# A hybrid transformer block on one core: its first stage as one pass over the input in blocks of k, and keys and queries put in place by ScalarE and VectorE

## The chip, the cores and the metric

One core of a Trainium2 chip runs the whole block; the other cores are idle. The metric is the device time of one execution in microseconds (us), and the median of several executions is compared. The engines are named as the profile names them: PE is TensorE's matmul, PEld its weight load, DVE is VectorE, ACT is ScalarE, POOL is GpSimd, SP is SyncE, which here only issues DMAs.

## The reference

One layer over 512 tokens of width 1024, batch 1, float32. Cut to what matters here:

```python
h = rms_norm(x, ln1_g)                       # x: 512 x 1024
z = h @ w_in                                 # 1024 x 3368; split into
# mq mk mv mo (512 each), mi mf (4 each), aq (512), akc avc aks avs akw avw (128 each), ag (24)
hm = mlstm(mq, mk, mv, mi + b_i, mf + b_f)   # 4 heads, gates by cumulative sums and maxima
m_out = rms_norm(hm) * sigmoid(mo)
# nsa: Kc = gelu(blocks(akc) + pos @ w1) @ w2, the same for Vc from avc (31 blocks of 32 tokens, stride 16);
# softmax attention over (Kc, Vc), over selected blocks (aks, avs) and over a window (akw, avw),
# 8 query heads in 2 groups, mixed by sigmoid(ag)
a_out = nsa(aq, akc, avc, aks, avs, akw, avw, ag, ...)
x = x + concat([m_out, a_out]) @ w_out
x = x + conv_ffn(rms_norm(x, ln2_g), w_up, conv_w, conv_b, w_down)
x = x + sigmoid(rms_norm(x) @ w_ple_gate) * (p @ w_ple_proj)
return rms_norm(x, final_g)
```

## The kernel before

Every matrix product of float32 data runs as three products of a high and a low part (`hi` by ACT `Copy` to fp32r, `lo` by a DVE subtraction): x-high by w-high, x-low by w-high, x-high by w-low. So each weight block that lands needs one ACT and one DVE instruction before TensorE can use it.

The activations stand transposed: eight blocks `k` of 128 features by 512 tokens (`x1h`, `x1l`). The work is a queue of jobs (`Stream`): a job loads a weight block (`split`, L119 to L126: a DMA on SP into one of two `raw` buffers, then hi, then lo), and its matmuls are written out while the next job's block is prepared. `st.after(us, fn)` writes a piece of other work (statistics, transposes, evacuations) after so many us of TensorE work have been written. A scheduler then fixes the order of instructions on each engine, and each engine runs its list strictly in that order.

The stages that the change touches, by their first matmul in the profile:

- `tok0` to `tok3` (L300, L301, L305): token-major products of 288 columns (v of two branches, gate inputs), a job for two blocks of k; the x blocks land and are split while these run. Then the squares and their sum `acc`, the statistics matmuls `n1ps` (L262), ten small DVE instructions (`newton_rsqrt`, L244 to L254), and `n1pb` (L281), which spreads the reciprocal norm over the columns as `rb1`.
- `c0`, `k0`, `c1` (L355, L356, L359): the feature-major products for akc, aks, avc, each 24 matmuls of 512 columns, one job each.
- `k1`, `q00`, then `cw00` (L434 to L439, the first layer of the compression, 24 small matmuls), `q01`, `cw01`, `mv0`, `cw10`, `mv1`, `cw11`, `mv2`, `mv3`: the order is the string `ORDER`. `pgt` (L579) and `pgc` (L600) are transposes for the mLSTM gates, whose chain of small operations runs over DVE and ACT (`mlstm_gates`, L579 to L593).
- Then the first scores (`s_3b`, L661) and the attention, into which `q10`, `q11`, `mo`, `mq` are filled; later the mLSTM heads, `w_out`, the FFN, the gate and the last norm.

A key or query has to stand twice, hi and lo, in rows of 64. `key_evac` and `q_evac` make hi and lo at 128 rows (L383, L384) and move the halves to their places by DMAs on POOL's queue (`move`, L388): 12 for the keys, 24 for the queries. `cmp_evac` shifts the two streams of the compression by one token through four DMAs on ACT's queue each (L411, L412) and adds the positions in four DVE sums (L418).

Of the kernel before, what the change touches and what calls it, by code (L numbers as in the profile page):

```python
# [39 lines left out]
GATES = "k0"  # L40
AHEAD = (1, 1)
# [25 lines left out]
def hybrid_block_kernel(ctx: ExitStack, tc: tile.TileContext, a, out):  # L67
# [40 lines left out]
    xbuf = main.tile([128, KB, S], F32, tag="B16", bufs=3, name="xT")  # L108
# [8 lines left out]
    def split(name, src_ap, shape):  # L117
        raw = wpool.tile(shape, F32, tag="raw", bufs=2, name=name + "r")
        hi = wpool.tile(shape, F32R, tag="hi", name=name + "h")  # L119
        lo = wpool.tile(shape, F32R, tag="lo", name=name + "l")  # L120
        n = 1 if name == "tok0" else shape[1]
        for i in range(0, shape[1], n):
            nc.sync.dma_start(raw[:, i:i + n], src_ap[:, i:i + n])
            SE.activation(hi[:, i:i + n], raw[:, i:i + n], AF.Copy)
            VE.tensor_sub(lo[:, i:i + n], raw[:, i:i + n], f32(hi[:, i:i + n]))
        return hi, lo  # L126

# [5 lines left out]
    class Stream:  # L133


        def __init__(self):
            self.jobs, self.ready, self.cur, self.done = [], [], None, set()
            self.now, self.events, self.debt = 0.0, [], 0.0
# [18 lines left out]
        def step(self):  # L157
            if self.cur is None:
# [5 lines left out]
                self.prepare(AHEAD[self.now > 100])  # L164
# [147 lines left out]

    psA = four("ptm")
    for c in range(4):
        st.add(f"tok{c}", a["w_tok"][:, 2 * c:2 * c + 2], [128, 2, 288], tokens_job(psA, 2 * c, 288))
    nc.sync.dma_start(cols, a["cols"])
    nc.sync.dma_start(xbuf[:, 0], a["xT"][:, 0])
    st.prepare(1)
    nc.sync.dma_start(xbuf[:, 1], a["xT"][:, 1])
    for c in range(4):  # L320
        if c < 3:
            nc.sync.dma_start(xbuf[:, 2 * c + 2:2 * c + 4], a["xT"][:, 2 * c + 2:2 * c + 4])
        for k in (2 * c, 2 * c + 1):
            last = SE.activation(xh[:, k], xbuf[:, k], AF.Copy, scale=cols[:, C_G1 + k:C_G1 + k + 1])
            VE.scalar_tensor_tensor(xl[:, k], xbuf[:, k], cols[:, C_G1 + k:C_G1 + k + 1], f32(xh[:, k]),
                                    op0=ALU.mult, op1=ALU.subtract)
        st.until(f"tok{c}")
        if c == 0:
            load_consts()
# [47 lines left out]
    mixa = main.tile([128, 2, 4, S], F32R, tag="mixa", name="mixa")  # L377
# [12 lines left out]
    def key_evac(br):  # L390
        def evac(ps):
# [832 lines left out]
```

## Time and profile before

| | us |
|---|---|
| median of 3 runs | 652.57 (648.09 to 653.72) |
| the profiled execution | 649.89 |
| its span, first to last instruction | 648.1 |
| PE busy in it | 621.4 (96%), 3090 matmuls |
| DVE, ACT, POOL busy | 422.3, 312.0, 51.8 |
| mean granted TensorE clock | 0.991 |

The profile is one execution. The span is 1.8 us less than the time of that execution. Busy shares are means over stages with different limits, so the stages are read one by one: the rows below begin with the whole and then go by stretches whose ends are the starts of a first matmul (5.75 `tok0`, 22.07 `c0`, 43.84 `k1`, 67.10 `mv0`, 95.71 the first scores).

### The profile page before, as it was taken

How to read it: one execution, taken by the hardware profiler on the slowest of the kernel's cores; microseconds unless marked ns; L12 is line 12 of the kernel's file. 1: busy time of each engine (PE TensorE's matmuls, PEld its weight loads, DVE VectorE, ACT ScalarE, POOL GpSimd, SP SyncE). 2: the span in 40 equal slices, each digit the busy share in tenths (PEclk: the TensorE clock that was granted, in tenths of full speed). 3: DMA queues.
4: the chain of work that ended last, by engine and by line, in shares of the span. 5: the costliest groups of instructions: out<-in, count | busy, mean ns of one | idle time of the engine just before them, and what ended most of it. 6: DMA issues, size and time to landing. Idle time of an engine off the chain costs nothing.

```text
span 648.1 us, 8626 instructions
## 1 busy us (share of the span) xinstructions
PE 621.4 (96%) x3090; PEld 506.6 (78%) x3090; DVE 422.3 (65%) x862; ACT 312.0 (48%) x650; POOL 51.8 (8%) x114
## 2 busy tenths in 40 slices
PE   6899899999999999999999999999999999999993
PEld 6788677777777777777878888888888888888892
DVE  4697548888877977685786555555555334346766
ACT  5544346677757656555545343433333323233642
POOL 1213104211111100000000000000000000000003
PEclk9999899999999999999999999999999999999997
DMA  7776945511211152113223323233233333333203
GB/s 226 183 177 159 217 130 114 115 33 33 66 36 63 34 195 89 42 34 97 66 97 98 97 98 98 98 98 98 98 98 98 98 97 98 98 99 108 87 2 129
DMA packets 22083, 64.85 MB, mean 100 GB/s; under 512 B 2832, under 2 KB 6032, under 8 KB 21844
## 3 DMA queue, kind: packets, MB, share of 16 engines
q1 hardware_dynamic: 18120, 57.55, 28.2%
q0 software_dynamic: 3136, 5.57, 4.7%
q10 hardware_dynamic: 784, 1.18, 0.7%
q8 instruction: 24, 0.39, 0.2%
q14 instruction: 19, 0.16, 0.1%
HBM read 56.42 MB, written 2.10 MB: 90 GB/s over the span
## 4 chain that ended last, share of the span: by engine, by line
PE 77%; DVE 10%; DMA 6%; ACT 4%; issue 2%; SPq 0%; DVEq 0%; POOL 0%; ACTq 0%
PE pu L355 8%; PE pu L359 8%; PE pu L356 8%; PE pd L355 5%; PE pd L356 5%; PE pd L359 5%; PE pt L711 2%; PE pmq L356 2%; DMA xT<-in_xT 2%; PE pmq L355 2%; PE pmq L359 2%; PE pv L719 1%; PE mo L889 1%; PE pg L347 1%; PE pg L348 1%
## 5 line engine op out<-in xcount | busy, mean ns | idle before, releaser
L1002 ACT ACTIVATE u<-zv 128x512 fp32r<-128x512 f32 x16 | 10.1, 633 | 45.3 <-DVE zv L1000 45.3
L714 ACT ACTIVATE ph<-pt 128x512 fp32r<-128x512 f32 x40 | 23.6, 597 | 16.4 <-PE pt L711 15.8
L999 DVE TENSOR_TENSOR zv<-pu,n2rb 128x512 f32<-128x512 f32 x16 | 11.1, 691 | 31.3 <-PE pu L359 31.3
L715 DVE TENSOR_TENSOR pl<-pt,ph 128x512 fp32r<-128x512 f32 x40 | 27.1, 684 | 6.3 <-ACT ph L714 6.0
L684 POOL TENSOR_SCALAR E<-E,rr 128x512 f32<-128x512 f32 (+3 forms) x32 | 20.4, 637 | 128.0 <-DVE rr L681 79.4
L989 DVE TENSOR_TENSOR zg<-pu,n2rb 128x512 f32<-128x512 f32 x16 | 11.1, 692 | 26.0 <-PE pu L359 24.6
L711 PE MATMUL pt<-ident,E 128*128 128x128 f32 x160 | 27.4, 274 | 0.4 <-DVE E L686 0.3
L1015 DVE TENSOR_TENSOR X<-pd,X 128x512 f32<-128x512 f32 x8 | 5.5, 691 | 31.9 <-PE pd L359 31.9
L711 PEld LDWEIGHTS pt<-ident,E 128*128 128x128 f32 x160 | 20.0, 140 | 6.7 <-DVE E L686 2.1
L992 ACT ACTIVATE cv<-zg,cols 128x512 f32<-128x512 f32 x16 | 13.1, 816 | 20.1 <-DVE zg L989 20.1
L678 ACT ACTIVATE E<-s,nm 128x384 f32<-128x384 f32 (+2 forms) x48 | 22.1, 470 | 0.0
L995 ACT ACTIVATE cv<-cv 128x512 f32<-128x512 f32 x16 | 10.1, 631 | 24.6 <-DVE cv L994 24.6
L988 POOL MEMSET zg<- 128x2 f32 x16 | 1.5, 99 | 244.0 <-DVE cv L994 151.0
L235 DVE TENSOR_TENSOR acc<-acc,sq 128x512 f32<-128x512 f32 (+1 forms) x30 | 19.1, 636 | 1.6 <-ACT sq L231 1.0
L719 PE MATMUL pv<-ph,V 128*128 128x512 f32 x40 | 18.7, 468 | 0.4 <-ACT ph L714 0.4
L231 ACT ACTIVATE sq<-X 128x512 f32<-128x512 f32 (+1 forms) x24 | 13.5, 560 | 11.0 <-DVE X L1056 11.0
L347 PE MATMUL pg<-x3h,wres 128*128 128x256 f32 x64 | 18.3, 285 | 0.0
L348 PE MATMUL pg<-x3l,wres 128*128 128x256 f32 x64 | 18.1, 283 | 0.0
L349 PE MATMUL pg<-x3h,wres 128*128 128x256 f32 x64 | 18.1, 283 | 0.0
L1003 DVE TENSOR_TENSOR u<-zv,u 128x512 fp32r<-128x512 f32 x16 | 11.1, 692 | 10.5 <-ACT u L1002 10.5
L1096 POOL TENSOR_TENSOR X<-X,n40rb 128x256 f32<-128x256 f32 (+1 forms) x5 | 4.8, 994 | 155.5 <-ACT n40rb L284 155.5
L721 PE MATMUL pv<-pl,V 128*128 128x512 f32 x40 | 16.7, 417 | 0.0
(1079 smaller groups left out, 2041.1 us busy)
## 6 DMA issues: line engine op xcount, KB each, us to landing
Q<-hlq POOLq DMA_DIRECT2D x24, 128.0 KB, 5.4
X<-in_xT SPq DMA_DIRECT2D x1, 2048.0 KB, 7.7
wgr<-in_w_pg SPq DMA_DIRECT2D x4, 512.0 KB, 4.0
xT<-in_xT SPq DMA_DIRECT2D x3, 512.0 KB, 6.4
K<-hlk POOLq DMA_DIRECT2D x12, 128.0 KB, 4.7
out_y<-X SPq DMA_DIRECT2D x5, 256.0 KB, 2.1
out_y<-X SPq DMA_DIRECT2D x5, 128.0 KB, 1.7
Q<-in_qaug POOLq DMA_DIRECT2D x2, 272.0 KB, 7.3
```

The source lines that it names most:

```text
L235: return VE.tensor_add(acc[:, :n], acc[:, :n], sq[:, :n])
L347: TE.matmul(ps, wh[:, kw], rh[:, kx, n], start=first, stop=False)
L348: TE.matmul(ps, wh[:, kw], rl[:, kx, n], start=False, stop=False)
L355: TE.matmul(ps, wh[:, w], rh[:, x, n], start=first and j == 0, stop=False)
L356: TE.matmul(ps, wh[:, w], rl[:, x, n], start=False, stop=False)
L359: TE.matmul(ps, wl[:, w], rh[:, x, n], start=False, stop=last and j == len(kx) - 1)
L678: SE.activation(e, p, AF.Exp, bias=nm[:, b:b + 1], accum_out=rs[:, b:b + 1])
L684: GE.tensor_scalar(e, e, rr[:, b:b + 1], 0.0, op0=ALU.mult, op1=ALU.add)
L711: TE.transpose(pt[:, r * 128:(r + 1) * 128], Es[r][:, c0:c0 + 128], ident)
L714: SE.activation(ph, pt, AF.Copy)
L715: VE.tensor_sub(pl, pt, f32(ph))
L719: TE.matmul(pv, vs, ph, start=first, stop=False)
```

## The change

- **One pass over k.** The 288 token-major columns and the columns of akc, aks and avc form one weight array `w_s1` of 672 columns for each block of k. Seven PSUM banks hold the sums (four of `ptm`, and `pc`, `pk`, `pc` for the three feature-major products). For k below `KO` = 4 all 21 products of a block follow one another; for k from 4 to 7 the products are done bank by bank: `pc` of akc, `n1ps`, `pk`, `pc` of avc with `n1pb` behind its first matmul, and last the 48 token-major ones. The scaling by ln1_g comes with x (a column of `xg`, whose rows are 514 words), the constants come in one DMA behind the first stage's loads, and nine matmuls of a zero tile stand ahead of all (`NWARM`).
- **Loads ahead.** Until `mv3` a block is loaded up to three jobs ahead of its split, into six buffers: four in the space of `mixa`, and the two `raw`.
- **No moves by DMA.** For the two keys and for the first group's queries (`q00`, `q01`) ACT copies 64 rows by 512 columns to each place and DVE subtracts there: four copies and two subtractions for a key, and the same for a pair of query heads. `cmp_evac` reads the shifted tokens from `z` itself in four DVE sums of 64 x 16 x 31. The second group's queries (`q10`, `q11`) are moved by POOL's DMAs as before.
- **Order.** `c0`, `k0`, `c1` leave `ORDER`; `mlstm_gates` is written 8 us (`T_GATES`) of TensorE work after the token-major evacuation, where it was written behind `k0`; `T_CT` goes from 6 to 8.

```diff
-ORDER = "c0 k0 c1 k1 q00 w00 q01 w01 m0 w10 m1 w11 m2 m3"
-T_TE = 4.0
+ORDER = "k1 q00 w00 q01 w01 m0 w10 m1 w11 m2 m3"
+W1 = 288 + 3 * 128
+KO = 4
+NWARM = 9
 T_GC = 14.0
-T_CT = 6
+T_GATES = 8.0
+T_CT = 8
...
+    nc.sync.dma_start(xbuf[:, 0], a["xg"][:, 0])
+    nc.scalar.dma_start(s1raw[0][:, 0, 0:288], a["w_s1"][:, 0, 0:288])
+    nc.sync.dma_start(s1raw[0][:, 0, 288:W1], a["w_s1"][:, 0, 288:W1])
+    for k, n in ((1, 1), (2, 2), (4, 2), (6, 2)):
+        nc.sync.dma_start(xbuf[:, k:k + n], a["xg"][:, k:k + n])
+        nc.sync.dma_start(s1raw[k], a["w_s1"][:, k:k + n])
+    nc.sync.dma_start(cols, a["cols"])
+    idle = s1.tile([128, 512], BF, name="idle")
+    VE.memset(idle, 0.0)
+    pidle = pV("idle")
+    for _ in range(NWARM):
+        TE.matmul(pidle, idle[:, 0:128], idle, start=True, stop=True)
...
+    pairs = ((xh, hi1), (xl, hi1), (xh, lo1))
     for k in range(KB):
-        sq = square(xbuf[:, k], k, acc1)
-        behind(sq, last, "the splits come first")
+        last = first_split(k)
+        if k > 1:
+            square(xbuf[:, k - 2, 0:S], k - 2, acc1)
+        if k < KO:
+            for x, w in pairs:
+                for t in range(NT):
+                    first_tok(k, t, x, w, k == 0 and w is hi1 and x is xh, False)
+            for x, w in pairs:
+                for j in range(3):
+                    first_feat(k, j, x, w, k == 0 and w is hi1 and x is xh, False)
...
+    def first_rest(j):
+        for x, w in pairs:
+            for k in range(KO, KB):
+                first_feat(k, j, x, w, False, k == KB - 1 and w is lo1)
+
+    first_rest(0)
     rc1 = rstd_stats(acc1, "n1")
...
-            zh, zl = parts_of(z, f"k{br}")
             for g in range(2):
-                gs = slice(g * 64, (g + 1) * 64)
-                move(K[0:64, g, 0, sl], zh[gs])
-                move(K[64:128, g, 0, sl], zh[gs])
-                move(K[0:64, g, 1, sl], zl[gs])
+                zg = z[g * 64:(g + 1) * 64]
+                for half in (g, 1 - g):
+                    SE.activation(K[half * 64:(half + 1) * 64, g, 0, sl], zg, AF.Copy)
+                VE.tensor_sub(K[0:64, g, 1, sl], zg, f32(K[g * 64:(g + 1) * 64, g, 0, sl]))
...
-            for g in range(2):
-                nc.scalar.dma_start(A[0:64, g], z[g * 64:(g + 1) * 64])
-                nc.scalar.dma_start(A[64:128, g, 0:S - 1], z[g * 64:(g + 1) * 64, 1:S])
...
+                blocks = bass.AP(zo.tensor, zo.offset, [zo.ap[0], [2, 16], [16, 31]])
+                VE.tensor_tensor(out=Xc[o * 64:(o + 1) * 64, :, g * 31:(g + 1) * 31], in0=blocks,
+                                 in1=pe[:, :, None].to_broadcast([64, 16, 31]), op=ALU.add)
...
+            if g == 0:
+                SE.activation(q[0:64, 0, e], z[0:64], AF.Copy)
+                SE.activation(q[64:128, 0, o], z[64:128], AF.Copy)
+                VE.tensor_sub(q[64:128, 0, e], z[0:64], f32(q[0:64, 0, e]))
+                VE.tensor_sub(q[0:64, 0, o], z[64:128], f32(q[64:128, 0, o]))
+                SE.activation(q[0:64, 1, e], z[0:64], AF.Copy)
+                SE.activation(q[0:64, 1, o], z[64:128], AF.Copy)
+                return
...
-    st.after(T_TE, token_evac)
-    st.until(GATES)
-    mlstm_gates()
-    st.after(T_GC, mlstm_gate_columns)
-    st.until("q01")
-    psM.extend(four("pmv"))
+    early[0] = main.tile([128, 4, 1024], F32, tag="mixa", name="rawx")
+    st.load(2)
+    first_rest(1)
+    rb1 = rstd_rows(rc1, "n1")
+    cmp_evac(0)(psF[0])
+    key_evac(0)(psF[1])
+    first_rest(2)
+    cmp_evac(1)(psF[2])
+    st.prepare(1)
+    st.load(LOADS)
+    for x, w in pairs:
+        for k in range(KO, KB):
+            for t in range(NT):
+                first_tok(k, t, x, w, False, k == KB - 1 and w is lo1)
+    token_evac()
+    st.after(T_GATES, mlstm_gates)
+    st.after(T_GATES + T_GC, mlstm_gate_columns)
```

How the instructions stand now, at three places. First, TensorE around the statistics (`pc` and `pk` are the banks of akc, aks and avc; `hi`, `lo` the parts of `w_s1`). Before:

```order
L355 MATMUL pc_328<-x1h,c0h 128x512
L356 MATMUL pc_328<-x1l,c0h 128x512
L359 MATMUL pc_328<-x1h,c0l 128x512 x5
L281 MATMUL n1pb<-ident,n1yc 128x128 x4
L359 MATMUL pc_328<-x1h,c0l 128x512 x3
L355 MATMUL pk_397<-x1h,k0h 128x512
L356 MATMUL pk_397<-x1l,k0h 128x512
```

TensorE in the change:

```order
L368 MATMUL pc_125<-x1h,lo_129 128x512 x4
L292 MATMUL n1ps<-ones_116,acc_121 128x1 x4
L368 MATMUL pk_126<-x1h,hi_128 128x512 x4
L368 MATMUL pk_126<-x1l,hi_128 128x512 x4
L368 MATMUL pk_126<-x1h,lo_129 128x512 x4
L368 MATMUL pc_127<-x1h,hi_128 128x512
L311 MATMUL n1pb<-cols,n1yc 128x128 x4
L368 MATMUL pc_127<-x1h,hi_128 128x512 x3
```

Before, `n1ps` stood inside `c0` and `n1pb` behind 12 more matmuls; now thirteen matmuls stand between the two, and half of the token-major work, which was done ahead of both, comes behind.

Second, ScalarE ahead of the split of `mv0` (`gt` is the mLSTM gates' row, `zq`, `hlq`, `Q` are the first queries). Before:

```order
L124 ACTIVATE cw00h<-cw00r 128x1024
L590 ACT_TABLE_LOAD
L590 ACTIVATE gt<-gt 4x512
L421 ACTIVATE cXh_503<-cX_498 128x992
L383 ACTIVATE hlk_540<-zk_538 128x512
L124 ACTIVATE q01h<-q01r 128x1024
L383 ACTIVATE hlq_594<-zq_592 128x512
L124 ACTIVATE cw01h<-cw01r 128x1024
L124 ACTIVATE mv0h<-mv0r 128x1024
```

ScalarE in the change:

```order
L152 ACTIVATE q01h<-q01r 128x1024
L642 ACTIVATE gt<-gt 4x512
L643 ACT_TABLE_LOAD
L643 ACTIVATE gt<-gt 4x512
L545 ACTIVATE Q_560<-zq_562 64x512
L546 ACTIVATE Q_560<-zq_562 64x512
L549 ACTIVATE Q_560<-zq_562 64x512
L550 ACTIVATE Q_560<-zq_562 64x512
L152 ACTIVATE cw01h<-cw01r 128x1024
L650 ACT_TABLE_LOAD
L650 ACTIVATE gt<-gt 4x512
L152 ACTIVATE mv0h<-rawx 128x1024
```

The gates' last exponential (L590 before, L650 now) stood six places ahead of the split of `mv0`, and now stands right ahead of it.

Third, VectorE in the gates' chain. Before:

```order
L584 SCALAR_TENSOR_TENSOR gf<-gf,gt 4x512
L586 SCALAR_TENSOR_TENSOR gt<-gf,zeroc 4x512
L587 TENSOR_TENSOR gi<-gi,gt 4x512
L588 SCALAR_TENSOR_TENSOR gf<-gi,zeroc 4x512
L589 TENSOR_TENSOR gt<-gt,gf 4x512
```

VectorE in the change:

```order
L640 TENSOR_SCALAR gf<-pgt_532,cols 4x512
L641 SCALAR_TENSOR_TENSOR gt<-gf 4x512
L542 SCALAR_TENSOR_TENSOR zq_562<-pq_508,n1rb 128x512
L153 TENSOR_TENSOR q01l<-q01r,q01h 128x1024
L644 SCALAR_TENSOR_TENSOR gf<-gf,gt 4x512
L547 TENSOR_TENSOR Q_560<-zq_562,Q_560 64x512
L646 SCALAR_TENSOR_TENSOR gt<-gf,zeroc 4x512
L548 TENSOR_TENSOR Q_560<-zq_562,Q_560 64x512
L647 TENSOR_TENSOR gi<-gi,gt 4x512
L153 TENSOR_TENSOR cw01l<-cw01r,cw01h 128x1024
L648 SCALAR_TENSOR_TENSOR gf<-gi,zeroc 4x512
L649 TENSOR_TENSOR gt<-gt,gf 4x512
```

From L644 on, two subtractions of the queries and the split of `cw01` now stand between the gates' own five instructions, which followed one another before.

## Rows read from the trace of the kernel before

**Rows 1.** The page's first part: busy us, share of the span and instructions of each engine; and from its second part TensorE's busy tenths in 40 slices of 16.2 us.

```profile
PE 621.4 (96%) x3090; PEld 506.6 (78%) x3090; DVE 422.3 (65%) x862; ACT 312.0 (48%) x650; POOL 51.8 (8%) x114
...
PE   6899899999999999999999999999999999999993
```

**Rows 2.** Busy time by stretches between first matmuls: stretch, its length, busy us of each engine (instructions), granted TensorE clock, mean busy share of the 16 DMA engines, GB/s.

```profile
0.00:5.75 5.75, 0.00 (x1) 0.00 (x1) 0.58 (x3) 2.59 (x5) 1.28 (x12) 1.00 0.56 172
5.75:22.07 16.32, 15.93 (x97) 15.51 (x97) 11.86 (x20) 11.96 (x20) 3.21 (x9) 1.00 0.85 246
22.07:43.84 21.77, 19.24 (x93) 15.19 (x93) 16.04 (x38) 7.66 (x12) 2.99 (x7) 1.00 0.61 161
43.84:67.10 23.26, 20.55 (x130) 16.93 (x128) 17.16 (x25) 11.30 (x14) 6.95 (x14) 0.99 0.80 176
67.10:95.71 28.61, 28.22 (x152) 22.62 (x153) 13.63 (x25) 9.90 (x18) 3.05 (x6) 0.95 0.69 178
95.71:648.00 552.29, 537.42 (x2623) 436.38 (x2621) 363.01 (x755) 268.62 (x586) 34.27 (x67) 0.99 0.27 85
```

**Rows 3.** Who waited for whom in the first 96 us: engine, tile and line, releaser; us in total, times, longest. The first three are all of TensorE's waits over 0.4 us there, the last is one of ScalarE's.

```profile
PE ptm L300 <- ACT tok0h L124: 5.7, 1, 5.7
PE pmv L300 <- ACT mv0h L124: 2.7, 1, 2.7
PE n1pb L281 <- issue: 2.5, 1, 2.5
...
ACT mv0h L124 <- DMA mv0r<-in_w_mv: 4.1, 1, 4.1
```

**Rows 4.** Three short stretches of TensorE, columns as in rows 2: the first matmuls (288 columns each), the ones behind them (288), and the ones behind the wait for `mv0` (512).

```profile
5.75:11.89 6.14, 6.14 (x24) 5.95 (x25) 3.16 (x6) 2.91 (x5) 0.70 (x1) 1.00 0.95 306
11.89:17.15 5.26, 5.26 (x41) 5.26 (x41) 4.58 (x9) 4.19 (x7) 0.88 (x2) 1.00 0.64 190
67.10:69.83 2.73, 2.73 (x7) 2.15 (x8) 2.73 (x3) 0.47 (x1) 1.65 (x4) 0.50 1.25 268
```

**Rows 5.** Instructions in order of time in `c0`: start, duration, engine, line, operation, shapes. Two matmuls of 512 columns in a row; the statistics and the matmul behind them; the first of the small DVE instructions and the spreading that waits for them.

```profile
22.63 0.39 PE L355 MATMUL pc<-x1h,c0h 128*128 128x512 f32 x1
22.86 0.39 PE L356 MATMUL pc<-x1l,c0h 128*128 128x512 f32 x1
...
24.43 1.05 PE L262 MATMUL n1ps<-ones,acc 128*128 128x1 f32 x8
25.35 0.48 PE L356 MATMUL pc<-x1l,c0h 128*128 128x512 f32 x1
...
28.56 0.15 DVE L268 TENSOR_SCALAR n1v<-n1ps 128x4 f32<-128x4 f32 x1
...
30.81 0.62 PE L281 MATMUL n1pb<-ident,n1yc 128*128 128x128 f32 x4 [2.47 <-issue]
```

**Rows 6.** Groups of instructions of the first 30 us by line and shape: busy us, mean ns of one, idle time before. The low part of x, the sum of squares, the two halves of a 1024-column split, and a 576-column one.

```profile
L325 DVE SCALAR_TENSOR_TENSOR x1l<-xT,cols,x1h 128x512 fp32r<-128x512 f32 x8 | 5.8, 754 | 6.2 <-ACT x1h L324 6.2
...
L235 DVE TENSOR_TENSOR acc<-acc,sq 128x512 f32<-128x512 f32 x7 | 4.8, 691 | 0.8 <-ACT sq L231 0.3
...
L125 DVE TENSOR_TENSOR k0l<-k0r,k0h 128x1024 fp32r<-128x1024 f32 x1 | 1.2, 1224 | 3.0 <-ACT k0h L124 3.0
...
L124 ACT ACTIVATE k0h<-k0r 128x1024 fp32r<-128x1024 f32 x1 | 1.1, 1061 | 4.3 <-DMA k0r<-in_w_in 4.3
...
L125 DVE TENSOR_TENSOR tok1l<-tok1r,tok1h 128x576 fp32r<-128x576 f32 x1 | 0.7, 746 | 0.0
```

**Rows 7.** Three stretches of the loads, columns as in rows 2; what counts here is the last column, GB/s.

```profile
2.00:9.00 7.00, 3.25 (x12) 3.09 (x13) 2.35 (x5) 2.33 (x6) 0.00 (x0) 1.00 0.84 250
9.00:12.00 3.00, 3.00 (x14) 2.97 (x14) 1.44 (x3) 1.91 (x3) 0.70 (x1) 1.00 1.02 370
2.00:30.00 28.00, 22.15 (x125) 20.19 (x125) 17.06 (x33) 14.98 (x26) 3.97 (x11) 1.00 0.79 219
```

**Rows 8.** The chain of the mLSTM gates in order of time, columns as in rows 5.

```profile
40.04 0.73 DVE L580 TENSOR_SCALAR gf<-pgt,gbias 4x512 f32<-4x512 f32 x1
...
43.29 0.67 DVE L581 SCALAR_TENSOR_TENSOR gt<-gf 4x512 f32<-4x512 f32 x1
...
44.33 0.61 ACT L582 ACTIVATE gt<-gt 4x512 f32<-4x512 f32 x1
...
44.96 1.28 ACT L583 ACT_TABLE_LOAD   x1
...
46.92 0.68 DVE L584 SCALAR_TENSOR_TENSOR gf<-gf,gt 4x512 f32<-4x512 f32 x1
...
47.63 1.21 DVE L586 TENSOR_TENSOR_SCAN gt<-gf,zeroc 4x512 f32<-4x512 f32 x1
...
48.88 0.68 DVE L587 TENSOR_TENSOR gi<-gi,gt 4x512 f32<-4x512 f32 x1
...
51.56 0.63 ACT L590 ACTIVATE gt<-gt 4x512 f32<-4x512 f32 x1 [0.46 <-DVE gt L589]
```

**Rows 9.** Groups by line and shape: a ScalarE copy of 64 rows by 512 columns, a VectorE subtraction of 512 columns, and the 248-column sums of `cmp_evac`, four for each of its two streams.

```profile
L725 ACT ACTIVATE os<-pv 64x512 f32<-64x512 f32 x8 | 4.8, 595 | 4.5 <-PE pv L721 4.5
...
L384 DVE TENSOR_TENSOR hlk<-zk,hlk 128x512 fp32r<-128x512 f32 x2 | 1.3, 671 | 0.0
...
L418 DVE TENSOR_TENSOR cX<-cA,cols 128x248 f32<-128x248 f32 x8 | 4.2, 568 | 0.0
```

More of the change, by code (lines that the diff above doesn't have):

```diff
@@ L115, in hybrid_block_kernel, with load, split @@
     GE.memset(epsc, EPS)
-    def split(name, src_ap, shape):
-        raw = wpool.tile(shape, F32, tag="raw", bufs=2, name=name + "r")
+    turn = [0]
+    def load(name, src_ap, shape):
+        raw = None
+        if early[0]:
+            turn[0] += 1
+            if turn[0] % 6 < 4:
+                raw = early[0][:, turn[0] % 6].rearrange("p (a b) -> p a b", a=shape[1])
+        if raw is None:
+            raw = wpool.tile(shape, F32, tag="raw", bufs=2, name=name + "r")
+        nc.sync.dma_start(raw, src_ap)
+        return raw
+    def split(name, raw, shape):
         hi = wpool.tile(shape, F32R, tag="hi", name=name + "h")
         lo = wpool.tile(shape, F32R, tag="lo", name=name + "l")
[L121 to L125, printed above, removed]
+        SE.activation(hi, raw, AF.Copy)
+        VE.tensor_sub(lo, raw, f32(hi))
         return hi, lo
+    early = [None]
     def behind(later, sooner, why, wait=False):
@@ L141, in add, with load @@
             self.jobs.append((name, src, shape, run))
+        def load(self, depth):
+            while len(self.loaded) < depth and self.jobs:
+                name, src, shape, run = self.jobs.pop(0)
+                self.loaded.append((name, load(name, src, shape), shape, run))
+                if name == "mv3":
+                    early[0] = None
         def prepare(self, depth):
-            while len(self.ready) < depth and self.jobs:
-                name, src, shape, run = self.jobs.pop(0)
-                self.ready.append((name, run, split(name, src, shape)))
+            while len(self.ready) < depth and (self.jobs or self.loaded):
+                self.load(1)
+                name, raw, shape, run = self.loaded.pop(0)
+                self.ready.append((name, run, split(name, raw, shape)))
         def after(self, us, fn):
@@ L163, in step @@
                 self.cur = (name, run(*w))
-                self.prepare(AHEAD[self.now > 100])
+                self.prepare(1)
+                if early[0]:
+                    self.load(LOADS)
             try:
@@ L313, in hybrid_block_kernel @@
     psA = four("ptm")
[L314 to L329, printed above, removed]
@@ L483, in evac @@
                 Q[g] = main.tile([128, 2, 4, S], F32R, tag="B16", bufs=3, name=f"Q{g}")
-                behind(nc.gpsimd.dma_start(Q[g][64:98, 1], a["qaug"][:, g]), last, "not needed early", True)
+                nc.gpsimd.dma_start(Q[g][64:98, 1], a["qaug"][:, g])
             q = Q[g]
@@ L602, in mlstm_gate_columns @@
         VE.tensor_copy(gcol, pt[:, 0:32].rearrange("p (a t h) -> p a t h", a=2, t=NT))
-    mstage = t2k("mstage")
-    nc.sync.dma_start(mstage[:, 0:128], a["mask"])
-    GE.tensor_copy(maskt, mstage[:, 0:128])
+    VE.tensor_copy(sel4, cols[:, C_SEL:C_SEL + 4])
+    GE.tensor_copy(maskt, cols[:, C_MASK:C_MASK + 128])
     GE.tensor_copy(identb, ident)
-    for g in range(2):
-        behind(nc.gpsimd.dma_start(K[64:98, g, 1, :], a["kaug"]), last, "not needed early", True)
     w2 = eb("w2", [128, 2, 128])
```

129 lines of the change are left out of this document (75 added, 54 removed).

## The prediction

> **What bounds the kernel now.** I read the page first: TensorE is busy for 621.4 of 648.1 us, no other engine for more than 422.3 [rows 1]. So the end is set by TensorE's work and by the places where it stands still. The stretches show where: behind 95.71 it stands for 552.29 − 537.42 = 14.9 us in the whole rest, of it some 11 in the last slice of 16.2, which is three tenths busy [rows 1], while ahead of it are 5.75 us before the first matmul, 2.5 us in the stretch from 22.07 and 2.7 us in that from 43.84 [rows 2]. The waits name them: 5.7 for the first weights, 2.5 at `n1pb`, 2.7 at `mv0` [rows 3]. `mv0` came late because ScalarE had waited 4.1 us for its DMA, and the wait cost more than itself: behind it the granted clock reads 0.50, the lower of the two levels, and seven matmuls take 2.73 us where the upper level's step of 0.23 gives 1.6 [rows 3 to 5]. A third cost has no wait: the first 24 matmuls of 288 columns take 6.14 us, 0.256 each, the next 41 take 5.26, 0.128 each [rows 4]. The granted clock is given as 1.00 in both, but the step doubles, so I read the first stretch as the lower level.
>
> The products themselves are the same before and after. What can be won is standing time and clock ahead of 95.71; from there the instructions follow in the same order but for some swaps in the first 20 us, and I carry any gain through to the end whole.
>
> **The first pass, part by part.** Before, `k1` starts at 43.84 [rows 2]. I work out the same point T for the change.
> - *First matmul.* It needs the first x block and 288 columns of weights, as before; the constants are no longer ahead. I take 5.5 for 5.75.
> - *Blocks 0 to 3.* Each has 12 matmuls of 288 columns at 0.13 and 9 of 512 at 0.23 [rows 4, 5]: 3.63 us, four make 14.5, to 20.0.
> - *The clock.* Nine idle matmuls of 512 columns at the lower level's 0.39 [rows 4] keep TensorE at work from about 1.2 to 5. Before, the step halved 6.1 us behind the first matmul. I take 0.5 us at the lower level behind 5.5: 20.5. Bounds: nothing, or 3.1 us if the idle matmuls don't count and 6.14 us run at half speed again.
> - *VectorE's side.* Per block: x-low 0.754, 672 columns of weights 0.87 (746 ns for 576, scaled), the sum of squares 0.691 [rows 6]: 2.31 us, so 17.8 for eight (the first has no sum). Starting at 4.8 with some 0.8 of early waits it ends at 23.4. TensorE has `pc` of akc done at 20.5 + 12 x 0.23 = 23.3, so `n1ps` goes at 23.4: here the two engines meet, and neither hides a slip of the other.
> - *Statistics.* `n1ps` takes 0.9 [rows 5], to 24.3; `pk` 2.8, to 27.1; one matmul of `pc`, 27.3. VectorE first does the splits of `k1` and `q00`, 2 x 1.22 [rows 6], to 25.9, then the chain to `n1pb`, 30.81 − 28.56 = 2.25 [rows 5], to 28.15. TensorE waits 0.85 (before: 2.5), `n1pb` 0.4, to 28.55.
> - *The rest.* 11 matmuls of 512 at 0.23 make 2.5, 48 of 288 at 0.13 make 6.3, changes between banks 0.4 by estimate: T = 37.8. Won so far: 43.84 − 37.8 = 6.0.
>
> **From `k1` to `mv0`.** Before 23.26 us, of them 2.7 waiting [rows 2, 3], so 20.6 of work. The eight small `pgc` go behind `mv0` (−0.6) and the two `pgt` come in (+0.8, less 0.3 of slow restarts): `mv0` is due at T + 20.5. The late loads are gone: the weights are issued up to three jobs ahead, and the moves through POOL's and ACT's queues no longer share the DMA engines. But `mv0`'s split now stands on ScalarE right behind the gates' last exponential, so the gates' chain decides. The second `pgt` ends at T + 10.6 (24 matmuls of `k1`, 19 of `q00`, two `pgt`). Then, each from [rows 6, 8, 9]: gf 0.73, gt 0.67, exponential 0.61, table 1.28, logarithm 0.61 (as the exponential), gf 0.68, query subtraction 0.67, scan 1.21, subtraction 0.67, gi 0.68, split of `cw01` 1.22, scan 1.21, sum 0.68, exponential 0.63, split of `mv0` 1.06: 12.6, with 14 handovers of 0.04 by estimate 13.2. `mv0` can start at T + 23.8, so TensorE waits 3.3 us. Queued behind that exponential on ScalarE are `mv0`, the second query copies and `cw10`, all with time to spare. The stretch comes to 23.8 for 23.26: 0.5 lost. Of this, 2.56 us are the three pieces put between the gates' own steps.
>
> The copies and sums that replace the DMAs: 16 ScalarE copies of 64 rows at 0.595 for four of 128 rows, eight VectorE subtractions at 0.67 for four [rows 9], and eight sums of 496 columns. The trace has none of 496; four of 248 with the same stride take 0.568 each [rows 9]. Bounds are 0.568 and twice that, 1.14; I take 0.75, near the 0.67 to 0.69 of a plain 512-column operation. All of it lies under TensorE's 12 us of `pc`, token products and `k1`, but only just: VectorE comes to `gi` at about T + 8.8, and the first `pgt` is there at T + 9.05. At 1.14 `gi`, and with it `mv0`, would be 2.9 us later; at 0.568 nothing changes. VectorE's 17.16 busy of 23.26 [rows 2] shows how full it was already.
>
> **From `mv0` to the first scores.** 28.61 before [rows 2]. A wait of 3.3 is longer than the 2.7 that left the clock at 0.50, so I keep that loss (2.73 − 1.6 = 1.1), add `pgc` 0.6, take off the small wait and the small product that fall out, 0.7: 28.5. Later: the second group's queries go the old way, and x is read again from rows that are not contiguous, both with room in the trace. I cost them at nothing; the load of x has some 17 us until its first use, so it could take three times as long.
>
> **Sum.** 6.0 − 0.5 + 0.1 = 5.6 us. For an execution like the profiled one 649.89 − 5.6 = 644.3. That execution is 2.7 below the median of 652.57, and 5.6 off the median gives 647.0.
>
> **Rivals.**
> *A, no wait at `mv0`.* If the gates' chain is out of the way, 3.3 and the 1.1 of clock come back: 10.0 won, 642.6. Against: every link has its row, and ScalarE's order is fixed. For: 13.2 us is a chain of fifteen links, and TensorE itself may be slower to `mv0` than I count, which would hide part of it.
> *B, the loads bind the pass.* Up to `q00`'s weights 6.19 MB must land: 4.86 of x and weights, 0.28 of constants, 1.05 of `k1` and `q00`. From that landing T is 1.06 + 1.22 + 2.25 + 0.4 + 2.5 + 6.3 + 0.4 = 14.1 us away. At the 250 GB/s of 2 to 9 us it lands at 26.8, T = 40.9, 2.5 won, 650.1. At the 219 of the first 28 us [rows 7] it lands at 30.3, T = 44.4, and the change is 1.0 slower: 653.6. From 227 GB/s down it loses. For it: blocks of 2,056 and 2,688 bytes a row. Against: 370 GB/s in 9 to 12 us [rows 7], when rows of 4,096 bytes were under way, and the 219 include stretches in which SP had nothing to issue; I have taken 285 or more, at which the loads are not last anywhere.
> The Trainium skill's page "DMA: Bandwidth & Descriptors" (How a descriptor splits into AXI transactions) speaks against the change here: a descriptor that doesn't start at a multiple of 256 bytes also fetches the bytes below its start. Rows of 2,056 bytes start anywhere; those of before, 2,048 and 4,096, start on it. By my estimate from that page the same bytes cost up to a tenth more, which at the 285 taken here would land `q00` near 26 and give T near 40, B's first case. No run shown so far has such rows.
> *C, the sums are slow.* At 1.14 us each the wait at `mv0` grows by 2.9: 2.7 won, 649.9.
> *D, the idle matmuls do nothing.* Then 3.1 us at the lower level, of which the 0.85 at `n1pb` and the 0.5 counted are absorbed: T near 39.5, 3.9 won, 648.7.
>
> **How the numbers follow.** Forecast (with D as its slow edge, and 0.5 us less clock and a shorter wait as its fast one: 3.9 to 7.8 won, 644.8 to 648.7) 0.52; A 0.22; B 0.16, of it 0.06 at or below 227 GB/s; C 0.10. A measurement of this kernel can tell about 1% from no change, 6.5 us. Faster by more: A, and not quite four tenths of the forecast, 0.42. Slower by more: the far end of B, 0.03. The rest 0.55. The range 640 to 652.5 reaches over A with the spread of the runs (652.57 − 648.09 = 4.5, about half of it below A's time) and over C and the first case of B; the slow end of B is left out.
>
> **What would show it.** Matmuls of 288 columns at 0.13 from about 6 us on (else D). `n1ps` near 23.4 and VectorE without a pause ahead of it; if ScalarE waits for the DMA of the last weight blocks or of `q00`, it is B. `k1` at 37 to 39. TensorE waiting some 3 us for `mv0`'s split with the gates' exponential ahead of it and the clock at 0.50 behind; no such wait is A. The 64 x 16 x 31 sums at 0.7 to 0.8 us (else C). First scores near 90. The forecast is wrong if the stretch behind the first scores changes by more than a microsecond, since I carry the gain through it untouched.

## The result and the profile after

The changed kernel takes 645.74 us in the median of 8 executions (645.48 to 647.65), the kernel before 651.67 (8 executions, 647.85 to 654.15): a ratio of 0.9932, 95% interval 0.9906 to 0.9958. By the bound of one per cent that is no difference; the interval says faster by 2.7 to 6.1 us. The profiled execution is one of 645.60, with a span of 643.8. Of the kernels further on, four to seven executions each, those of one kernel lie 0.5 to 3.2 us apart, but for a single one of 1249.65 (the sums in steps of two columns), of which there is no trace. By stage (us, from the two traces and from the prediction's working):

| | before | after | forecast |
|---|---|---|---|
| first matmul | 5.75 | 5.64 | 5.5 |
| `k1` starts | 43.84 | 37.06 | 37.8 |
| `k1` to `mv0` | 23.26 | 25.31 | 23.8 |
| `mv0` to the first scores | 28.61 | 28.79 | 28.5 |
| first scores | 95.71 | 91.16 | 90.1 |
| from there to the end of the span | 552.4 | 552.6 | unchanged |
| the profiled execution | 649.89 | 645.60 | 644.3 |

So 6.8 us are won up to `k1`, 2.1 are given back before `mv0`, 0.2 behind it and 0.25 behind the first scores. Of the 6.8, 0.1 is the earlier first matmul, 2.8 are standing time between it and `k1` (2.9 before, 0.1 now), and 3.9 are busy time of TensorE, for the greater part in the first 24 matmuls of 288 columns: 3.6 us (5.64 to 7.60 and 9.69 to 11.29), where they took 6.14 [rows 4]. No run undoes the one pass or the loads ahead by itself, so how much each of them brought is not shown. The same stretches in the trace, beside [rows 2]: stretch, its length, busy us of PE, PEld, DVE, ACT and POOL (instructions), granted clock, DMA share, GB/s. The next line is the time at the lower clock behind the wait for `mv0` (it begins 1.1 us behind the wait's end, and seven matmuls start in it), to be read beside the last of [rows 4]; the last two are the loads, beside [rows 7].

```profile
5.64:20.69 15.05, 15.04 (x85) 13.27 (x85) 14.18 (x22) 14.41 (x25) 1.20 (x3) 1.00 0.95 379
20.69:37.06 16.37, 16.26 (x97) 14.37 (x96) 14.51 (x28) 5.23 (x9) 5.60 (x15) 1.00 0.54 187
37.06:62.37 25.31, 20.78 (x130) 16.86 (x128) 22.66 (x35) 16.21 (x23) 0.51 (x1) 1.00 0.23 74
62.37:91.16 28.79, 28.79 (x158) 22.94 (x158) 14.38 (x27) 11.73 (x18) 0.00 (x0) 0.94 0.17 55
91.16:643.80 552.64, 538.16 (x2626) 436.43 (x2624) 363.42 (x757) 268.64 (x588) 35.03 (x67) 0.99 0.27 85
...
63.43:66.41 2.98, 2.98 (x8) 2.31 (x7) 2.89 (x5) 2.85 (x5) 0.00 (x0) 0.50 0.02 5
...
2.00:12.00 10.00, 9.56 (x45) 6.52 (x44) 5.99 (x10) 7.50 (x15) 0.00 (x0) 1.00 0.98 352
9.00:17.00 8.00, 8.00 (x46) 7.12 (x45) 7.48 (x12) 8.00 (x14) 0.00 (x0) 1.00 1.02 415
```

The first pass has next to no standing time left: 31.3 us of TensorE in 31.4. The stretch from 37.06 has 4.5, and in it VectorE is busy for 22.7 of 25.3 us where it was 17.2 of 23.3. TensorE's waits over 0.5 us up to the first scores, beside [rows 3] (engine, tile and line, releaser; us, times, longest):

```profile
PE pmv L332 <- ACT mv0h L152: 2.8, 1, 2.8
PE pgt L639 <- DVE gi L640: 1.5, 1, 1.5
PE idle L127 <- DVE ones L247: 1.2, 1, 1.2
```

The wait at `mv0` was forecast at 3.3, the one at the second `pgt` at none; the last stands ahead of the idle matmuls and costs nothing. The instructions that make them, and the statistics of the first pass, in order of time (start, us, engine, line, operation, shapes, idle time before and what ended it):

```profile
1.19 4.02 PE L127 MATMUL idle<-idle 128*128 128x512 bf16 x9 [1.19 <-DVE ones L247]
5.64 0.79 PE L364 MATMUL ptm<-hi,x1h 128*128 128x288 f32 x4 [0.44 <-ACT x1h L353]
...
22.19 0.68 DVE L265 TENSOR_TENSOR acc<-acc,sq 128x512 f32<-128x512 f32 x1
...
23.48 0.95 PE L292 MATMUL n1ps<-ones,acc 128*128 128x1 f32 x8
...
27.69 0.62 PE L311 MATMUL n1pb<-cols,n1yc 128*128 128x128 f32 x4
...
30.18 4.11 DVE L473 TENSOR_TENSOR cX<-zc,cols 64x496 f32<-64x496 f32 x4
...
37.59 4.09 DVE L473 TENSOR_TENSOR cX<-zc,cols 64x496 f32<-64x496 f32 x4
...
48.13 0.74 DVE L640 TENSOR_SCALAR gi<-pgt,cols 4x512 f32<-4x512 f32 x1
48.93 0.60 PE L639 MATMUL pgt<-cols,gz 128*4 128x128 f32 x4 [1.49 <-DVE gi L640]
...
60.74 0.63 ACT L650 ACTIVATE gt<-gt 4x512 f32<-4x512 f32 x1 [2.26 <-DVE gt L649]
61.28 1.04 ACT L152 ACTIVATE mv0h<-rawx 128x1024 fp32r<-128x1024 f32 x1
62.37 0.50 PE L332 MATMUL pmv<-mv0h,x1h 128*128 128x512 f32 x1 [2.76 <-ACT mv0h L152]
```

Eight sums take 8.2 us of VectorE ahead of `gi`; so `gi` comes at 48.13 although the first `pgt` ends at 46.3, the second `pgt`, whose bank `gi` has to read first, waits, and 12.8 us of chain behind it end in `mv0`'s split, which stands behind the gates' exponential.

### The profile page after: what moved, and what is told of

It reads as the page before. It is cut to its first block, busy times and chain, and to the rows that moved or that the text cites. A ratio compares the mean times of both kernels' runs of the same rounds, so it can differ in the third digit from the quotient of the medians.

```text
span 643.8 us, 8563 instructions
## 1 busy us (share of the span) xinstructions
PE 623.0 (97%) x3099; PEld 505.1 (78%) x3099; DVE 429.9 (67%) x868; ACT 318.8 (50%) x663; POOL 42.7 (7%) x92
## 4 chain that ended last, share of the span: by engine, by line
PE 82%; DVE 10%; ACT 4%; issue 1%; DMA 1%; DVEq 0%; ACTq 0%
PE pu L415 8%; PE pu L419 8%; PE pu L416 8%; PE pd L415 5%; PE pd L416 5%; PE pd L419 5%; PE pt L784 2%; PE pmq L416 2%; PE pmq L415 2%; PE pmq L419 2%; PE pv L792 2%; PE pmv L332 1%; PE pg L407 1%; PE ms L953 1%; PE pc L368 1%
## 5 line engine op out<-in xcount | busy, mean ns | idle before, releaser
L1072 DVE TENSOR_TENSOR zv<-pu,n2rb 128x512 f32<-128x512 f32 x16 | 11.1, 691 | 31.3 <-PE pu L419 31.3
L784 PE MATMUL pt<-cols,E 128*128 128x128 f32 x160 | 27.8, 275 | 0.4 <-DVE E L759 0.3
L784 PEld LDWEIGHTS pt<-cols,E 128*128 128x128 f32 x160 | 20.0, 140 | 7.2 <-DVE E L759 2.6
L741 DVE TENSOR_REDUCE nm<-s 128x2 f32<-128x768 f32 (+2 forms) x24 | 16.4, 682 | 0.0
```

Source lines behind the costliest of these rows:

```text
L784: TE.transpose(pt[:, r * 128:(r + 1) * 128], Es[r][:, c0:c0 + 128], ident)
```

## The experiments

Each kernel is an edit of the changed one, and times are medians to be held against its 645.74. What is below a microsecond is read from the traces, of which there is one for each run.

**The changed kernel once more.**

> The changed kernel once more, unchanged, beside the other two. Theory (its time hangs on one wait and one fall of the clock, and its first pass on where the clock rises): 645.7, wait at mv0 2.8, wait at pgt 1.5; the first pass either as seen (n1ps at 23.5) or, if the clock rises later behind the idle matmuls, up to 2 us later and the time with it.

Measured: 645.83; waits of 2.8 and 1.5 again, `k1` at 36.94. But behind the same wait the clock did not fall:

```profile
62.26:66.20 3.94, 3.94 (x17) 3.28 (x18) 3.85 (x6) 3.71 (x6) 0.00 (x0) 1.00 0.01 4
```

`mv0` to the first scores took 27.17 and not 28.79. The 1.6 us were not kept: at the first `pu`, near 319, TensorE waited 1.1 us for VectorE's part of `wu00`, and from the first scores to the end it took 554.2 instead of 552.6. So a stage is known to some 0.3 us from one trace, but for these two places and, as the next run says, the start of the first pass.

**Without the idle matmuls** (rival D).

```diff
-NWARM = 9
+NWARM = 0
```

> The nine idle matmuls ahead of the first pass are left out; nothing else differs. Theory (they are what lets the first pass start near the upper clock): the first matmuls of 288 columns run at 0.25 us for several microseconds, as before the change, the first block ends 2 to 3 us later than 9.7, n1ps moves from 23.5 to about 25.8, k1 from 37.1 to about 39.2, and the whole time from 645.7 to about 647.8. Rival 1 (the clock rises by itself at the same time): first block and time unchanged, 645.7. Rival 2 (the pass is bound by VectorE, which ends its splits at 22.8 whatever TensorE does): the first block is later, but n1ps by less than 1 us and the time by less than 1 us.

Measured: 647.03, `n1ps` at 24.79, `k1` at 38.08. The first four matmuls, as in the rows above:

```profile
5.75 1.33 PE L364 MATMUL ptm<-hi,x1h 128*128 128x288 f32 x4 [5.75 <-ACT x1h L353]
```

The lower level lasts until about 9 us; it is read from the steps, which are doubled, for the granted clock reads 1.00 here as it does in [rows 4]. The theory holds with about half its price: 1.3 us in the median, 1.0 at `k1`. It isn't a guarantee: in two of twelve profiled executions with the idle matmuls (the next experiment's and the one with the filled wait) the first pass ran at the lower level, again by its steps, until about 10 us all the same.

**`mv0`'s split ahead of the gates' exponential.** `held` keeps the instruction of a split by its name, and `behind(a, b, ...)` puts a behind b in the order of their engine.

```diff
...
-        SE.activation(gt_, gt_, AF.Exp, scale=-1.0)
+        st.after(9.5, lambda: behind(SE.activation(gt_, gt_, AF.Exp, scale=-1.0), held['mv0'], 'mv0 first'))
```

> ScalarE's order alone is changed: the split of mv0 stands ahead of the gates' last exponential and not behind it. Theory (the gates' chain is what TensorE waits for at mv0): the wait of 2.8 us goes, mv0 starts near 59.7 and not at 62.4, the granted clock behind it stays at 1.00 where it was 0.50 (1.1 to 1.4 us more), and TensorE waits at most 0.3 for the low half of mv0 on VectorE: 3.6 to 4 us in all, 641.7 to 642.1. Rival 1 (something else is late there too, the weights or VectorE): a wait of over 1 us stays at mv0, 643.5 to 645. Rival 2 (the fall of the clock does not come from the wait): the wait goes, the clock falls all the same, 643.

Measured: 645.02. The wait at `mv0` is gone (22.39 us from `k1` to `mv0`), so the gates' chain, through its exponential ahead of the split, was its cause. The wait at `pgt` stays, and TensorE now waits a little later, behind `mv0`:

```profile
PE pgt L639 <- DVE gi L640: 1.5, 1, 1.5
PE pmv L332 <- ACT mv1h L152: 1.4, 1, 1.4
...
PE pmv L337 <- DVE mv0l L153: 0.4, 1, 0.4
```

The clock read 1.00 in the 4.8 us behind `mv0`. Of the 3.6 to 4 us expected the trace shows 2.2 from `k1` to the first scores; in this execution the first pass also began at the lower clock (`k1` at 38.80). What was queued on VectorE and ScalarE behind the chain is next late.

**Four of the sums on GpSimd.**

```diff
-                VE.tensor_tensor(out=Xc[o * 64:(o + 1) * 64, :, g * 31:(g + 1) * 31], in0=blocks,
+                (GE if g == o else VE).tensor_tensor(out=Xc[o * 64:(o + 1) * 64, :, g * 31:(g + 1) * 31], in0=blocks,
```

> Four of the eight 64 x 496 sums go to GpSimd, which has nothing to do there; VectorE keeps four of 1.02 us. Theory (VectorE comes late to gi because the sums take 1.02 and not 0.75): gi starts 1.5 us sooner or more, the wait of 1.5 us at the second pgt goes, the gates' chain starts 1.5 us sooner and mv0 with it, its wait stays near 2.8: 644.2. Rival (GpSimd's sums take over 2 us each, or hold VectorE up while both work): the copies and low parts that need them come late, a wait at the first compressed products takes the place of the one at pgt: 645.5 to 648.

Measured: 644.69, `k1` to `mv0` 25.05, the wait at `pgt` still 1.1. By tile (count; shortest, median, longest in ns):

```profile
L473 POOL TENSOR_TENSOR cX<-zc,cols x4: 1293/1306/1865, 29.4 to 39.2; 64x496 f32<-64x496 f32 x4
L473 DVE TENSOR_TENSOR cX<-zc,cols x4: 1005/1293/1915, 30.0 to 42.6; 64x496 f32<-64x496 f32 x4
```

While GpSimd works, VectorE's two sums take 3.5 us together, and 2.0 when it doesn't: most of the relief is lost. The Trainium skill's page "GPSIMD Engine Reference" (1. Specifications) says that GpSimd shares its SBUF interfaces with VectorE and contends with VectorE instructions of two SBUF inputs; the trace agrees.

**Plain sums** (rival C's term by itself).

```diff
-                blocks = bass.AP(zo.tensor, zo.offset, [zo.ap[0], [2, 16], [16, 31]])
+                blocks = bass.AP(zo.tensor, zo.offset, [zo.ap[0], [31, 16], [1, 31]])
```

> The eight sums read 496 neighbouring columns of z and not every sixteenth one, so what the compressed streams are made of is no longer the reference's blocks; sizes, counts and order stay. Theory (the gather is what makes a sum 1.02 us): a sum takes 0.66 like other VectorE operations of 512 columns, VectorE comes to gi 2.9 us sooner, the wait of 1.5 us at the second pgt goes, mv0 starts 1.5 us sooner and still waits 2.8: 644.2, or 642.6 if the clock doesn't fall behind that wait. Rival (the second operand, repeated along the columns, is what costs): a sum stays at 1.0 and nothing moves, 645.7.

Measured: 644.25, no wait at `pgt`, `k1` to `mv0` 23.66, wait at `mv0` 2.8, clock fallen behind it. The group (busy us, mean ns):

```profile
L473 DVE TENSOR_TENSOR cX<-zc,cols 64x496 f32<-64x496 f32 x8 | 5.4, 670 | 0.1
```

The theory to the tenth: the gather costs 0.35 us a sum, and 1.5 us of the time hang on it. With plain sums `mv0` comes 23.7 us behind `k1`, as forecast.

**Placed by DMA again** (that part of the change undone alone: `key_evac`, the first queries and `cmp_evac` as before).

```diff
-                for half in (g, 1 - g):
-                    SE.activation(K[half * 64:(half + 1) * 64, g, 0, sl], zg, AF.Copy)
...
+                move(K[0:64, g, 0, sl], zh[gs])
...
+                nc.scalar.dma_start(A[0:64, g], z[g * 64:(g + 1) * 64])
```

> The first pass stays as changed; the compressed inputs, keys and first queries are put in place by DMA again, as before the change (two copies of z by ScalarE's queue and 128 x 248 sums; 128-row splits and moves by GpSimd's queue). Theory (placing by ScalarE and VectorE costs and doesn't pay): k1 stays at 37.1, VectorE is some 4 us lighter ahead of gi, the wait of 1.5 us at pgt goes, the gates' chain is 0.7 us shorter, mv0 waits some 2 us: 643.4. Rival (the DMAs were what made the stretch late before): the compressed products or the first scores wait for landings, or the weights behind them come late, 646 to 650.

Measured: 645.10, `k1` at 36.91, `k1` to `mv0` 26.67. Both theory and rival fall: the sums are cheaper, but VectorE stands still for their input, and the gates come later, not sooner (TensorE waits 3.5 us at the two `pgt`, 2.3 at `mv0`).

```profile
DVE cX L477 <- DMA cA<-zc: 7.0, 3, 4.5
```

So within the new pass the placing by ScalarE and VectorE is worth 1.4 us of this stretch. In this profile the clock stayed up behind `mv0` (27.17 to the first scores), which is why the two spans, 643.6 and 643.8, are so near. On the whole time the placing shows no gain at all: without it the median is 0.6 us lower. All that is won lies ahead of `k1`.

**Aligned rows** (rival B).

```diff
-    xbuf = main.tile([128, KB, S + 2], F32, tag="B16", bufs=3, name="xT")
+    xbuf = main.tile([128, KB, S], F32, tag="B16", bufs=3, name="xT")
...
 W1 = 288 + 3 * 128
+WR = W1 + 32
...
```

> Rows of x are 2,048 bytes again (the gains come by a small transfer of their own ahead of them), rows of the first weights are padded from 2,688 to 2,816 bytes, so that every row starts at a multiple of 256 bytes; the padding is loaded and not used. Theory 1 (the skill's rule that a row off such a boundary costs up to a tenth more): from 2 to 12 us the loads run at some 385 GB/s and not at 352, the last weights land 1 us sooner. Theory 2 (what the trace of the changed kernel suggests, since it already has the rate of the best stretch before): the rate stays within 3% of 352. In both the time is 645.7 within half a microsecond, because the loads are not last.

Measured: 648.26. The first matmul waits 0.4 us longer behind the small transfer, and `n1pb` 0.4 more; another 1.5 us lie behind the first scores, for the most part from the first `pu` on, as in the repeat of the changed kernel; what makes them is not shown. By the sizes of the rows, almost all rows of x and every second row of the weights start off a boundary in the changed kernel, and none here. What the run was for is the rate: 344 GB/s from 2 to 12 us for 352, and, beside the last line of the stretches of the changed kernel:

```profile
9.00:17.00 8.00, 8.00 (x47) 7.09 (x46) 7.06 (x12) 7.26 (x13) 0.00 (x0) 1.00 1.02 415
```

The same 415 GB/s with rows on and off a 256-byte boundary: theory 2. The rule cited in the prediction, from the Trainium skill's page "DMA: Bandwidth & Descriptors" (How a descriptor splits into AXI transactions), shows no price here that this could measure.

**Gates sooner, the second stream's sums later.**

```diff
-T_GATES = 8.0
+T_GATES = 4.0
+T_SUMS = 24.0
...
-    cmp_evac(1)(psF[2])
+    cmp_evac(1, T_SUMS)(psF[2])
```

Two of the late sums are tied behind the gates' first steps on VectorE, two behind `mv0`'s low half.

> Nothing is left out, two orders change: the gates start 4 us sooner, and the four sums of the second compressed stream stand behind the gates' first steps (two) and behind the low half of mv0 (two) on VectorE. Theory (the wait at mv0 is the gates' chain, and it starts late because the sums stand ahead of it): no wait at pgt, mv0 starts 20.8 us behind k1 with no wait, the clock stays up, first scores 27.2 us behind mv0 and not 28.8: k1 37.1, mv0 57.9, first scores 85 to 86, 639.5 to 640.5. Rival (VectorE itself is the bound of the stretch, 22.7 of 25.3 us busy): what was put off makes cw01, mv0 or w10's low halves late by 2 us or more together, 642 to 643.5.

Measured: 643.76, `k1` to `mv0` 23.75, no fall of the clock, VectorE busy for 21.3 of the 23.75. TensorE's waits behind `k1`:

```profile
PE pq L416 <- ACT q01h L153: 1.5, 1, 1.5
...
PE pc L503 <- DVE cw01l L154: 0.8, 1, 0.8
PE pc L499 <- DVE cXl L487: 0.7, 1, 0.7
PE pmv L333 <- ACT mv1h L153: 0.5, 1, 0.5
```

Nearer to the rival, but not as it was put. The waits at `pgt` and `mv0` are gone, as the theory had it; low parts from VectorE come 1.5 us late together (`cw01` 0.8, `cXl` 0.7), less than the rival's 2; and 1.5 more is ScalarE's split of `q01`, which neither named. The same work in another order makes other pieces late.

**The wait filled with matmuls.**

```diff
                 ps.extend(four("pmv"))
+                fill = pV("fill")
+                for _ in range(11):
+                    TE.matmul(fill, xh[:, 0, 0:128], xh[:, 0], start=True, stop=True)
```

> Eleven matmuls of 512 columns, 2.5 us, whose result nobody reads, stand ahead of mv0, where TensorE otherwise waits 2.8 us. Theory (standing still is what lets the clock fall behind the wait): the wait shrinks to some 0.3, mv0 starts where it did, the granted clock behind it stays at 1.00, first scores come 27.2 us behind mv0 and not 28.8: 644.1. Rival (the fall comes from something else): the clock reads 0.50 behind mv0 as before, 645.7.

Measured: 644.84; the wait is 0.2, the clock 1.00 behind it, 27.20 us from `mv0` to the first scores; its first pass began at the lower clock (`k1` at 38.45). It fits the theory but does not prove it, since three unfilled waits of 2.3 to 2.8 us (the repeat, GpSimd's and the DMA run) had no fall either, against five that had (before, after, without idle matmuls, plain sums, aligned rows). None of the five other kernels, whose wait there is 1.0 or less, had one.

**Sums in steps of two columns.**

```diff
-            Xc = ea(f"cX{kv}", [128, 16, 62])
+            Xc = ea(f"cX{kv}", [128, 62, 16])
...
-                blocks = bass.AP(zo.tensor, zo.offset, [zo.ap[0], [2, 16], [16, 31]])
+                blocks = bass.AP(zo.tensor, zo.offset, [zo.ap[0], [16, 31], [2, 16]])
...
-                TE.matmul(pc[0:62, 0:128], Xh[:, jj], wh[:, j], start=(jj == 0), stop=False)
+                TE.matmul(pc[0:62, 0:128], Xh[:, :, jj], wh[:, j], start=(jj == 0), stop=False)
```

> Nothing is left out. The compressed streams lie in SBUF with the 16 columns of one block side by side and not the 31 blocks, so that a sum runs through z in steps of two columns inside and of sixteen outside; instead TensorE's weights for the compressed products are read in steps of sixteen columns. Theory (long steps of the inner loop are what costs): a sum takes 0.67 us as with neighbouring columns, the wait at the second pgt goes, mv0 starts 23.7 us behind k1 as with the plain sums, 644.2, and the products of the compressed streams keep their 0.06 us each. Rival 1 (any step over one costs): a sum stays at 1.02, nothing moves, 645.7. Rival 2 (the cost only moves to the weight loads): the 96 products of the four compressed jobs take longer, 0.1 us each would be 4 us, 646 to 648.

Measured: 645.12. A sum takes 0.67 us, the wait at `pgt` is gone, `mv0` 23.66 us behind `k1`; and each of the four compressed jobs now takes some 2.6 us instead of 1.4, because a weight load takes

```profile
L489 PEld LDWEIGHTS pc<-cw00h,cXh 128*62 128x62 f32 x8 | 1.6, 202 | 0.0
```

where the changed kernel has

```profile
L489 PEld LDWEIGHTS pc<-cw00h,cXh 128*62 128x62 f32 x8 | 1.0, 133 | 0.0
```

Rival 2, in part behind a wait (the one at `mv0` is down to 1.0). The step of 16 columns costs the engine that reads it, VectorE there and TensorE here.

**That layout with two splits moved.** The edit of the second experiment, and the split of `mv1` ahead of the first compressed stream's tanh, whose chain is written 7.5 us of TensorE work later for it.

```diff
...
+        if kv == 0:
+            behind(i, held['mv1'], 'mv1 first')
...
```

> Nothing is left out. The layout of the run before, and ScalarE's order: the split of mv0 ahead of the gates' last exponential, the split of mv1 ahead of the first compressed stream's tanh. Theory (with VectorE 2.9 us lighter, the two splits are the last things that TensorE waits for here): no wait over 0.4 us from k1 to the first scores, no fall of the clock, mv0 21 us behind k1, first scores 27.2 to 27.6 behind mv0: 37.1 + 21 + 27.4 + 552.6, a span of 638.1, 639.9 in all. Rival (VectorE stays the bound behind mv0): the low halves of mv0, cw10 or mv1 come 1 us or more late, 641 to 642.5.

Measured: 644.76, no wait over 0.4 us from `k1` to the first scores and no fall of the clock, but `k1` to `mv0` 22.54 and from there 29.37. The span of 641.6 is 3.5 us longer than expected; the slower compressed jobs of this layout, some 1.2 us more in each of four, would make more than that. That they are the whole of it is not shown.

**The gates behind `mv1`.**

```diff
-T_GATES = 8.0
+T_GATES = 24.0
```

> One number differs from the changed kernel: the gates start 24 us and not 8 us behind the first pass by the kernel's own clock, so that their chain stands behind the split of mv1 on ScalarE and VectorE and its transposes within the second compressed job. Theory (the gates' chain, 7 us of VectorE's work and two exponentials, is what fills the stretch from k1 to mv0, and nobody needs its result before the mLSTM): no wait at mv0, the clock stays up, mv0 20.2 us behind k1 (25.3 less 2.8, 1.5, 0.3 and the 0.7 of the transposes), first scores 27.8 to 28.5 behind mv0, where the transposes stand now, and a gain of 5 us at the first scores; behind these 0 to 1.5 us are lost again at the first pu, as in other executions: 639.5 to 641.5. Rival (the chain is late wherever it stands): a wait of 2 us or more at the second pgt, at mv2's halves or at the first scores, 643 or more.

Measured: 641.18 (640.41 to 641.68), ratio to the kernel before 0.9831 (0.9793 to 0.9869): 4.6 us under the changed kernel, the fastest of all. Stretches from `k1` and from `mv0`, and the only wait over 0.5 us in them:

```profile
37.42:56.74 19.32, 19.32 (x122) 16.34 (x121) 16.03 (x26) 12.39 (x19) 0.51 (x1) 1.00 0.32 91
56.74:86.22 29.48, 28.16 (x170) 22.49 (x168) 20.99 (x36) 15.57 (x23) 0.00 (x0) 1.00 0.19 58
```

```profile
PE pgt L639 <- DVE gi L640: 1.3, 1, 1.3
```

The theory, within its range. TensorE stands nowhere between `k1` and `mv0`. VectorE has 16.0 us of work there instead of 22.7, the rest where it had 14.4. First scores come at 86.22, 4.9 sooner; 1.0 is lost again behind them.

## Why the prediction was right, point by point

- *First matmul, blocks 0 to 3.* 5.64 for 5.5 and 20.69 for 20.5. The clock cost 0.4 us of the 0.5 I took. My price for the idle matmuls' failure, 3.1 us from [rows 4] and 1.7 of it left at `k1`, was too high: leaving them out cost 1.0 at `k1`, since the lower level then lasted some 3.5 us and not the 6.1 of before. Why it was shorter is not shown.
- *VectorE's side of the pass.* It ended at 22.8, not 23.4; `n1ps` at 23.48 hung on TensorE alone. `n1pb` came at 27.69 for 28.15, TensorE's wait there, counted by steps as I had, is 0.3 for 0.85, and `k1` came at 37.06 for 37.8. Of these 0.7 us, 0.5 are from this term; the rest is mainly the 0.4 for changes between banks, which no row had shown, and of which the trace shows nothing.
- *Loads.* 352 GB/s from 2 to 12 us where the forecast needed 285, and TensorE did not stand still for a load in the pass: B was far off. I had weighed rates of stretches in which little was issued.
- *The sums.* **The mis-sized term.** I took 0.75, near a plain 512-column operation; they took 1.02. The right row was there: four of 248 columns with the same step at 0.568 [rows 9]; twice that is the 1.14 of my upper bound, and 1.02 lies nearer to it than to 0.75. The mechanism was rival C's, and by my own sign (0.7 to 0.8, else C) so was the outcome, at half of C's price: 1.5 us and not 2.9, since the sums took 2.2 more than I had counted and part of that lay within VectorE's slack.
- *The gates' chain.* 12.8 us from the end of the second `pgt` to `mv0`, forecast 13.2; TensorE's wait 2.8, forecast 3.3; ScalarE's exponential ahead of `mv0`'s split, as said. Rival A is out.
- *The clock behind the wait.* Fallen to 0.50 as in [rows 4]; cost 1.6 (28.79 against the 27.2 of executions without it), forecast 1.1. That it falls is not certain, as the repeat shows; I had taken it as fixed.
- *Behind the first scores.* 0.25 us longer where I assumed no change, though across the kernels of this study the stretch varied from 552.5 to 554.2, with the first `pu` as one place.
- *The sum.* 4.3 us between the two profiled executions, 5.6 forecast: 0.8 more up to `k1`, 1.5 less before `mv0`, 0.3 less up to the first scores, 0.25 less behind them. The mechanism held, and the one large miss is the sums. The medians differ by 5.9, and the predicted 647.0 is within 1.3 of the measured 645.74; that this gain lies nearer to the forecast than that of the two traces is luck, since the profiled execution of before was 1.8 below its median and that of after at its own. Executions of before lie 4 to 9 us apart in each set of 7 to 11, and their mean granted clock goes with the time: of the 36 whose clock was read, 0.984 to 0.989 in the ten above 653, 0.989 to 0.994 in the nine below 650.7. The twelve of after read 0.990 to 0.993. That the change thereby also took away falls of the clock is a reading of these numbers, not shown by a trace.

## What to carry to other kernels

When a pass is made shorter, look at which engine becomes full in the stretch behind it: here VectorE went from 74 to 90 per cent and the stretch gave back three tenths of the gain, and moving a chain that nobody was waiting for out of that stretch won more (4.6 us) than making any piece of it cheaper (1.5). Price an operation by the row that has its access pattern, not by the one that has its size.

## What the runs showed of the hardware

- In these runs the step of the innermost loop sets the price of reading SBUF: 496 columns of float32 take VectorE 0.67 us in steps of one or two columns and 1.02 in steps of sixteen; a weight load of 62 columns takes TensorE 133 ns in steps of one and 202 in steps of sixteen. The Trainium skill's page "SBUF — State Buffer" (Door 1: The DMA port swizzle) speaks of lines of 16 bytes that are read at full rate only when at least two accesses in a row fall into one; both numbers agree with that. A look at it would have spoken against the price of a plain operation for the sums, though the page gives no figure there.
- The same wait of 2.8 us was followed by a fall of the granted clock to 0.50 in one profiled execution of the changed kernel and by none in another. Over all kernels, waits of 2.3 to 2.8 us there had a fall behind them in five traces of eight, of 2.7 to 3.4 us each.
